# Two weight slabs in turns behind a norm, and where the squares are added: a hybrid encoder on one core

## The chip, the core and the metric

The kernel runs on one core of one Trainium2 chip. The metric is the time of one execution on the device in microseconds (us); the median of several runs is given. The engines are named as the profile names them: PE (TensorE, matrix products; PEld is its loading of weights), DVE (VectorE), ACT (ScalarE), POOL (GpSimd) and SP (SyncE, which issues most transfers).

## The reference

A two-layer encoder over 512 tokens of width 1024, in float32:

```python
def hybrid(x):                                     # [1, 512, 1024]
    x = x + stick_breaking_attention(rms_norm(x, norm_mix[0]), w_qkv, w_o)
    x = x + squared_relu_mlp(rms_norm(x, norm_mlp[0]), mlp_w1[0], mlp_w2[0])
    x = x + rglru_block(rms_norm(x, norm_mix[1]), ...)   # w_in, conv, gates, scan, w_o
    x = x + squared_relu_mlp(rms_norm(x, norm_mlp[1]), mlp_w1[1], mlp_w2[1])
    return rms_norm(x, norm_final)

def rms_norm(x, g):
    return x * rsqrt(mean(x * x, axis=-1) + 1e-6) * g

def squared_relu_mlp(h, w1, w2):                   # w1 1024x4096, w2 4096x1024
    u = relu(h @ w1)
    return (u * u) @ w2
```

## The kernel before, in words

Everything is kept transposed: the stream x is 8 chunks `x[0]` to `x[7]` of 128 channels by 512 tokens. A weight matrix is read in slabs of 1024 inputs by 128 outputs (512 KB). For precision every operand is split into two halves, a rounded one (`wh`, `xgh`, `bh`) and the rest (`wl`, `xgl`, `bl`), and each product is three matmuls (`three`, lines 187 to 191). So one slab (`dense`, line 193) is 8 steps over the chunks k = 0 to 7 with 3 matmuls each, 24 in all, into one PSUM bank.

`slab` (line 168) issues the slab's transfer on SP's queue (line 172), casts `wh` on ACT (line 178) and subtracts `wl` on DVE (line 184). There are four buffers of `wh` and `wl`.

The norm does not stand in front of the next product. `residual` (line 626) finishes the layer: for each chunk c it runs the last slab's product, adds it to `x[c]` (`add_x`, DVE, line 624), writes the halves of x times the norm's gain (`halves`: `xgh` on ACT, line 117; `xgl` on DVE, line 118), and squares the chunk (`Squares.chunk`: Square on ACT, lines 135 and 138, added up into `ssq` on POOL, line 139). Two buffers hold squares. The next layer's first products start from the halves; the factor 1/rms is applied to their results. It comes from `Squares.inv_rms` (line 141): one product of `ssq` with ones on PE (line 143), a square root on ACT and a reciprocal on DVE (lines 123 and 124).

`residual` is called at three seams: attention's end to the first MLP (line 635, gain `mlp0`), the first MLP's end to the recurrent layer (line 824), and the recurrent layer's end to the second MLP (line 1000). At attention's end the products of chunks 0 to 6 are nearly done beforehand (`so`), and only chunk 7 is a whole slab.

The MLP's `squared` (line 675) makes one slab of w1, then scales by `r`, applies the ReLU (DVE, line 684) and squares (ACT, line 685). Its first call also makes `r`, behind its own slab. Two slabs make a pair: four sums on DVE (line 699), a split into halves on ACT (line 715) and DVE (line 716), after which `u`, of one buffer, is free for the next pair. Eight slabs are followed by the first two of the next quarter, and then by `down` (line 736), whose first product reads pairs 0 and 1 (`bh`, `bl`) and then pairs 2 and 3 (`sh`, `sl`). Eight PSUM banks go round in the order `oottaazz`.

The recurrent layer's `dense_in` (line 893) makes one slab of w_in; `conv(0)` calls it first, and that first call makes `r`, behind its own slab.

The order of work: a scheduler orders the instructions of each engine by a priority (program order) and by when its own model takes them to be ready. Inside `manual_schedule(engines={PE})` PE's instructions keep the order in which they are written, but where such a region falls among PE's other instructions stays the scheduler's choice. `high_priority()`, put around each `conv` (line 986), makes instructions come first as soon as they are ready. `issue_after(ins)` queues a block's instructions behind `ins`.

Of the kernel before, what the change touches and what calls it, by code (L numbers as in the profile page):

```python
# [11 lines left out]
F32 = mybir.dt.float32  # L12
F32R = mybir.dt.float32r
AF = mybir.ActivationFunctionType
ALU = mybir.AluOpType
PSUM = bass.MemoryType.PSUM

P = 128
S = 512
D = 1024  # L20
C = D // P
# [26 lines left out]
def hybrid_encoder(  # L48
# [24 lines left out]
    V, A, G, PE = nc.vector, nc.scalar, nc.gpsimd, nc.tensor  # L73
# [3 lines left out]
    work = ctx.enter_context(tc.tile_pool(name="work", bufs=2))  # L77
# [5 lines left out]
    def bank(tag=None):  # L83
        if tag is None:
            tag = TAGS[turn[0] % len(TAGS)]
            turn[0] += 1
        return psum.tile([P, S], F32, tag=tag, name=f"ps_{tag}")

    def f(ap):
        return ap.bitcast(F32)  # L90
# [4 lines left out]
    def col(name):  # L95
        o, n = COLS[name]
        return colt[:, o : o + n]
# [10 lines left out]
    xgh = const.tile([P, C, S], F32R, tag="xgh", name="xgh")  # L108
    xgl = const.tile([P, C, S], F32R, tag="xgl", name="xgl")
# [4 lines left out]
    def halves(gname, c, xc):  # L114

        g = col(gname)[:, c : c + 1]
        A.activation(xgh[:, c, :], xc, AF.Identity, scale=g)  # L117
        V.scalar_tensor_tensor(xgl[:, c, :], xc, g, f(xgh[:, c, :]), ALU.mult, ALU.subtract)  # L118

    def inv_rms(ps):  # L120

# [5 lines left out]
    class Squares:  # L127
# [2 lines left out]
        def __init__(self):  # L130
            self.acc = work.tile([P, S], F32, tag="ssq", name="ssq", bufs=1)

        def chunk(self, c, xc):
            if c == 0:
                A.activation(self.acc, xc, AF.Square)
            else:
                sq = work.tile([P, S], F32, tag="sq", name="sq")
                A.activation(sq, xc, AF.Square)
                G.tensor_tensor(self.acc, self.acc, sq, ALU.add)

        def inv_rms(self):
            ps = bank("z")
# [25 lines left out]
    def slab(src, cut=1, ks=range(C)):  # L168
        raws = rawpools[next(loads) % len(rawpools)]
        raw = raws.tile([P, C, P], F32, tag="raw", name="raw", bufs=3 if raws is wpool else 1)  # L170
        k = slice(ks.start, ks.stop)
        nc.sync.dma_start(out=raw[:, k, :], in_=src[:, k, :])
        pool = wpools[next(slabs) % len(wpools)]
        wh = pool.tile([P, C, P], F32R, tag="wh", name="wh")
        wl = pool.tile([P, C, P], F32R, tag="wl", name="wl")
        for i in range(cut):
            k = slice(ks.start + i * len(ks) // cut, ks.start + (i + 1) * len(ks) // cut)
            A.copy(wh[:, k, :], raw[:, k, :])  # L178
            if adding[0]:

                G.tensor_scalar(wl[:, k, :], f(wh[:, k, :]), -1.0, None, ALU.mult)
                G.dma_start(out=wl[:, k, :], in_=raw[:, k, :], accum_op=ALU.add)
            else:
                V.tensor_tensor(wl[:, k, :], raw[:, k, :], f(wh[:, k, :]), ALU.subtract)  # L184
        return wh, wl

    def three(ps, ah, al, wh, wl, start, stop):

        PE.matmul(ps, wh, ah, start=start, stop=False)  # L189
        PE.matmul(ps, wl, ah, start=False, stop=False)  # L190
        PE.matmul(ps, wh, al, start=False, stop=stop)  # L191

    def dense(src, ah, al, tag=None, halves=None, ks=range(C), ps=None):

        wh, wl = halves or slab(src, ks=ks)
        ps = bank(tag) if ps is None else ps
        for k in ks:
            three(ps, ah[:, k, :], al[:, k, :], wh[:, k, :], wl[:, k, :], k == ks[0], k == ks[-1])
        return ps


    NB = S // P
# [2 lines left out]
    so, early = {}, {}  # L205
# [4 lines left out]
    def home_tile(tag, n, name):  # L210
        return home.tile([P, S], F32, tag=tag, name=name, bufs=n)

    with ExitStack() as actx:
# [19 lines left out]
        for i in range(2):  # L233
            both = []
            for nm in ("h", "l"):
                t = sp.tile([P, 2 * P], F32R, tag=f"last{nm}{i}", name=f"last{nm}{i}")
# [74 lines left out]
        first = [bank("acc") for _ in range(2)]  # L311
# [6 lines left out]
        with tc.manual_schedule(engines=others):  # L318
# [13 lines left out]
            for kind, c in START:  # L332
# [4 lines left out]
                else:  # L337
                    A.activation(sqs[c], xcs[c], AF.Square)
                    if c > 1:
                        e, acc = ((G, sums), (V, odd))[c % 2]  # L340
# [125 lines left out]
        turns = [0]  # L466
# [124 lines left out]
        for i in range(n_fill):  # L591
# [5 lines left out]
            if i == LATE:  # L597
                x = [home_tile(tag, n, "x") for tag, n in HOMES[:7]]
# [16 lines left out]
        for c in range(C - 1):  # L615
            for _ in so_more(c, C - 1):
                pass
            if c == 0:
                so_next = {C - 1: slab(w_so[C - 1], CUT)}
# [3 lines left out]
    def add_x(c, ps):  # L623
        V.tensor_tensor(x[c], x[c], ps, ALU.add)

    def residual(srcs, gname, begun={}, ready={}):

        sq = Squares()
        for c in range(C):
            add_x(c, begun[c][0] if c in begun else dense(srcs[c], bh, bl, halves=ready.get(c)))  # L630
            halves(gname, c, x[c])
            sq.chunk(c, x[c])
        return sq

    sq = residual(w_so, "mlp0", so, so_next)


    NQ = DFF // D
# [3 lines left out]
    class Mlp:  # L642
# [31 lines left out]

        def squared(self, q4, c):

            ps = dense(w_m1[self.layer, q4 * C + c], xgh, xgl, ps=self.bank())
            if self.r is None:
                self.r = self.sq.inv_rms()
            j, a = divmod(c, 2)  # L680
            if a == 0:
                self.u[j] = self.mp.tile([P, PIECES, HS], F32, tag="u", name="u", bufs=1)
            t = self.u[j][:, 2 * a : 2 * a + 2, :].rearrange("p i n -> p (i n)")
            V.scalar_tensor_tensor(t, ps, 0.0, self.r, ALU.max, ALU.mult)  # L684
            A.activation(t, t, AF.Square)  # L685
            return t
# [118 lines left out]
    with ExitStack() as mctx:  # L805
        mctx.enter_context(tc.manual_schedule(engines={mybir.EngineType.PE}))
        mlp = Mlp(mctx, 0, sq)
        back = count()

        def between(q4, c):  # L810

            if q4 < NQ - 1 or c < 4:
                return
            for c in islice(back, 2):
                pt = mlp.bank()
                for t in range(NB):
                    PE.transpose(
                        pt[:, t * P : (t + 1) * P], mlp.y(t, c // 4)[:, c % 4 * P : (c % 4 + 1) * P],
                        ident,
                    )  # L820
                add_x(c, pt)

        mlp.quarters(between)
        sq = residual(w_m2, "mix1")
# [8 lines left out]
    with ExitStack() as rctx:  # L833
# [32 lines left out]
        for i in range(2):  # L866
            t = rp1.tile([P, 2, P], F32, tag=f"graw{i}", name=f"graw{i}")
# [15 lines left out]
        r = None  # L883
# [5 lines left out]

        xc, aa, om, z, hs, gin = {}, {}, {}, {}, {}, {}  # L890
        turns = [0, 0]

        def dense_in(i):

            nonlocal r
            adding[0] = turns[0] >= 6
            ps = dense(w_in[i], xgh, xgl, tag=("acc", "t")[turns[0] % 2])
            turns[0] += 1
            if r is None:
                r = sq.inv_rms()  # L900
            return ps

        def conv(c):

            ps = dense_in(C + c)
            V.tensor_tensor(ps, ps, r, ALU.mult)
            aa[c], xc[c], om[c] = (
                rp1.tile([P, S], F32, tag=t, name=t, bufs=n)
                for t, n in (("aa", 5), ("bt", 6), ("om", C))
            )  # L910
            x0 = xc[c]
            nonlocal begin, tap, high, low
            taps = [cw[:, i * C + c : i * C + c + 1] for i in range(4)]
            begin = A.activation(x0, ps, AF.Identity, bias=col("conv_b")[:, c : c + 1], scale=taps[3])
            for d in range(1, 4):
                tap = V.scalar_tensor_tensor(
                    x0[:, d:], ps[:, : S - d], taps[3 - d], x0[:, d:], ALU.mult, ALU.add
                )

            i = C - 3 + c % 3  # L920
            xch, xcl = bh[:, i, :], bl[:, i, :]
            high = A.copy(xch, x0)
            low = V.tensor_tensor(xcl, x0, f(xch), ALU.subtract)
            gin[c] = (xch, xcl, *gate_weights(c))
# [39 lines left out]
        def gate(c):  # L964
            ps = dense_in(c)
            z[c] = rp1.tile([P, S], F32, tag="z", name="z", bufs=6)
            V.tensor_tensor(z[c], ps, r, ALU.mult)
# [23 lines left out]
        begun = {}  # L991
        for c in range(4):
            wh, wl = slab(w_ro[c])
            begun[c] = bank("oozz"[c]), wh, wl
        for k in range(C):
            for c in range(4):
                ps, wh, wl = begun[c]
                three(ps, bh[:, k, :], bl[:, k, :], wh[:, k, :], wl[:, k, :], k == 0, k == C - 1)

    sq = residual(w_ro, "mlp1", begun)  # L1000
    wctx.close()
    wpools[:], rawpools[:] = [wpool], [wpool]


    with ExitStack() as mctx:
# [24 lines left out]
        for h in range(2):  # L1030
            ws = []
            for k in range(C // 2):
                raw = wpool.tile([P, C, P], F32, tag="raw", name="raw", bufs=3)
                nc.sync.dma_start(out=raw, in_=w_last[h, k])
                wh = lw.tile([P, C, P], F32R, tag="wh", name="wh")
                A.copy(wh, raw)
                wl = lw.tile([P, C, P], F32R, tag="wl", name="wl")
                V.tensor_tensor(wl, raw, f(wh), ALU.subtract)
                ws.append([t.rearrange("p (k f) e -> p k (f e)", k=2) for t in (wh, wl)])
            for t in range(NB):  # L1040
# [3 lines left out]
                for i, (e0, e1) in enumerate(units):  # L1044
                    ps = bank()[:, : e1 - e0]
                    for k in range(C):
                        wh, wl = (w[:, k % 2, e0:e1] for w in ws[k // 2])
# [4 lines left out]
                    g = gb[:, h * S + e0 : h * S + e1]  # L1052
# [11 lines left out]
                last = len(units)  # L1064
# [83 lines left out]
```

## Time and profile before

| what | value |
|---|---|
| runs, us | 1099.35, 1099.39, 1102.22 |
| median, us | 1099.39 |
| profiled execution, us | 1099.0 |
| its span, us | 1097.3 |
| mean granted clock of PE | 0.996 |
| PE / DVE / ACT / POOL busy, us | 1075.0 / 772.1 / 563.4 / 216.7 |

The span runs from the first to the last instruction of the profiled execution. A timeline row gives the start, the duration, the engine, the line of the kernel, the operation and what it writes and reads, and in brackets the idle time before it and what ended that. Matmuls are pipelined: a row's duration is from issue to end, so the distance of two starts is what one costs. A row of the list of waits gives who waited for whom: us in total, times, the longest. A row of busy time by stretch gives the stretch, its length, and each engine's busy time with the number of instructions, then PE's granted clock, the share of the DMA engines and GB/s.

### The profile page before, as it was taken

To read this page: it belongs to the slowest core of one execution; us is meant where nothing else is said; L and a number is where in the kernel's file an instruction comes from. 1 tells how busy PE (TensorE), PEld (TensorE's weight loads), DVE (VectorE), ACT (ScalarE), POOL (GpSimd) and SP (SyncE) were. 2 spreads that over 40 slices of the span, in tenths; PEclk is the share of its full clock that TensorE was granted. 3 is DMA by queue.
4 is the path that set the end of the run, shared out by engine and by line. 5 is a ranking of instruction groups with operands and counts; after the bars stand their busy time and mean duration, and the time that the engine had idled before them with its cause. 6 is when DMAs were issued, how large, how long until landed. Compare 5 with 4: busy or idle time off the path is not lost.

```text
span 1097.3 us, 13621 instructions
## 1 busy us (share of the span) xinstructions
PE 1075.0 (98%) x5052; PEld 890.0 (81%) x5052; DVE 772.1 (70%) x986; ACT 563.4 (51%) x831; POOL 216.7 (20%) x228
## 2 busy tenths in 40 slices
PE   9999999998999999999999999999999999999997
PEld 7888888886888888888888788888888888888886
DVE  7777787838784597699565648975684697699522
ACT  6766776726445444344344467854455444443422
POOL 2344344533000000000222555122000000002220
PEclk9999999999999999999999999999999999999999
DMA  7744354436205305301334476242205205303402
GB/s 236 196 108 136 103 147 107 137 100 216 94 20 173 116 20 171 116 20 56 118 108 135 103 183 144 96 168 90 88 31 183 95 22 186 99 1 103 165 1 77
DMA packets 43170, 122.57 MB, mean 112 GB/s; under 512 B 7648, under 2 KB 8416, under 8 KB 43104
## 3 DMA queue, kind: packets, MB, share of 16 engines
q1 hardware_dynamic: 41088, 115.94, 33.9%
q0 software_dynamic: 1440, 5.24, 2.6%
q8 instruction: 40, 0.66, 0.2%
q10 hardware_dynamic: 576, 0.52, 0.2%
q14 instruction: 26, 0.21, 0.1%
HBM read 101.76 MB, written 2.10 MB: 95 GB/s over the span
## 4 chain that ended last, share of the span: by engine, by line
PE 91%; DVE 4%; DMA 2%; ACT 1%; issue 1%; SPq 1%; POOL 0%; DVEq 0%; ACTq 0%; POOLq 0%
PE ps_acc L189 7%; PE ps_acc L190 7%; PE ps_acc L191 7%; PE ps_o L191 4%; PE ps_t L190 4%; PE ps_t L189 4%; PE ps_t L191 4%; PE ps_o L189 4%; PE ps_o L190 4%; PE ps_z L190 3%; PE ps_z L189 3%; PE ps_z L191 3%; PE ps_t L758 2%; PE ps_t L757 2%; PE ps_t L759 2%; PE ps_acc L758 2%
## 5 line engine op out<-in xcount | busy, mean ns | idle before, releaser
L178 ACT CAST wh<-raw 128x1024 fp32r<-128x1024 f32 (+2 forms) x144 | 128.4, 910 | 156.0 <-PE ps_acc L191 51.3
L184 DVE TENSOR_TENSOR wl<-raw,wh 128x1024 fp32r<-128x1024 f32 (+2 forms) x134 | 146.0, 1103 | 30.9 <-ACT wh L178 30.8
L690 POOL TENSOR_TENSOR bl<-u,bh 128x512 fp32r<-128x512 f32 x16 | 28.2, 1761 | 559.4 <-ACT bh L689 541.5
L189 PE MATMUL ps_acc<-xgh,wh 128*128 128x512 f32 x320 | 128.3, 401 | 1.3 <-ACT xgh L117 1.1
L732 ACT CAST wh<-b 128x1024 fp32r<-128x1024 f32 x72 | 75.5, 1049 | 102.4 <-PE ps_acc L759 16.2
L191 PE MATMUL ps_acc<-xgl,wh 128*128 128x512 f32 x320 | 125.8, 393 | 0.6 <-DVE xgl L118 0.6
L190 PE MATMUL ps_acc<-xgh,wl 128*128 128x512 f32 x320 | 126.0, 394 | 0.2 <-DVE wl L160 0.2
L733 DVE TENSOR_TENSOR wl<-b,wh 128x1024 fp32r<-128x1024 f32 x72 | 87.9, 1221 | 27.1 <-ACT wh L732 27.1
L493 DVE TENSOR_TENSOR_SCAN scan<-keep,later 128x128 f32<-128x128 f32 (+1 forms) x64 | 56.9, 890 | 22.9 <-ACT keep L485 14.4
L191 PEld LDWEIGHTS ps_acc<-xgl,wh 128*128 128x128 f32 x320 | 60.4, 189 | 14.6 <-DVE xgl L118 1.5
L189 PEld LDWEIGHTS ps_acc<-xgh,wh 128*128 128x128 f32 x320 | 60.5, 189 | 12.8 <-ACT xgh L117 1.8
L190 PEld LDWEIGHTS ps_acc<-xgh,wl 128*128 128x128 f32 x320 | 60.5, 189 | 10.8 <-DVE wl L160 0.8
L685 ACT ACTIVATE u<-u 128x512 f32<-128x512 f32 x64 | 39.6, 630 | 54.4 <-DVE u L684 54.2
L189 PE MATMUL ps_t<-xgh,wh 128*128 128x512 f32 x168 | 66.1, 394 | 0.0
L497 POOL TENSOR_TENSOR w<-w,scan 128x128 f32<-128x128 f32 (+1 forms) x64 | 54.9, 858 | 56.4 <-DVE scan L493 55.0
L190 PE MATMUL ps_t<-xgh,wl 128*128 128x512 f32 x168 | 65.7, 391 | 0.0
L191 PE MATMUL ps_t<-xgl,wh 128*128 128x512 f32 x168 | 65.5, 390 | 0.0
L191 PE MATMUL ps_o<-xgl,wh 128*128 128x512 f32 x152 | 60.3, 397 | 3.9 <-DVE xgl L118 3.9
L189 PE MATMUL ps_o<-xgh,wh 128*128 128x512 f32 x152 | 61.1, 402 | 0.0
L190 PE MATMUL ps_o<-xgh,wl 128*128 128x512 f32 x152 | 59.7, 393 | 0.0
L189 PE MATMUL ps_z<-xgh,wh 128*128 128x512 f32 x128 | 50.0, 391 | 0.0
L190 PE MATMUL ps_z<-xgh,wl 128*128 128x512 f32 x128 | 49.9, 390 | 0.0
(339 smaller groups left out, 2783.4 us busy)
## 6 DMA issues: line engine op xcount, KB each, us to landing
raw<-in_w_m SPq DMA_DIRECT2D x72, 512.0 KB, 3.5
b<-in_w_dn SPq DMA_DIRECT2D x36, 512.0 KB, 4.3
raw<-in_w_in SPq DMA_DIRECT2D x16, 512.0 KB, 3.5
raw<-in_w_qk SPq DMA_DIRECT2D x12, 512.0 KB, 3.8
raw<-in_w_dn SPq DMA_DIRECT2D x12, 512.0 KB, 3.5
wl<-raw POOLq DMA_DIRECT2D x10, 512.0 KB, 5.3
x<-in_xT SPq DMA_DIRECT2D x16, 256.0 KB, 4.1
raw<-in_w_ro SPq DMA_DIRECT2D x8, 512.0 KB, 3.5
```

Source lines behind the costliest of these rows:

```text
L178: A.copy(wh[:, k, :], raw[:, k, :])
L184: V.tensor_tensor(wl[:, k, :], raw[:, k, :], f(wh[:, k, :]), ALU.subtract)
L189: PE.matmul(ps, wh, ah, start=start, stop=False)
L190: PE.matmul(ps, wl, ah, start=False, stop=False)
L191: PE.matmul(ps, wh, al, start=False, stop=stop)
L493: V.tensor_tensor_scan(sc[:, S - n : S][:, ::-1], keep[:, :n][:, ::-1], later[:, S - n :][:, ::-1], 1.0, ALU.mult, ALU.max,)
L497: G.tensor_tensor(wt, wt, sc[:, S - n + 1 : S + 1], ALU.mult)
L685: A.activation(t, t, AF.Square)
L690: G.tensor_tensor(bl[:, c, :], t, f(bh[:, c, :]), ALU.subtract)
L732: A.copy(wh, raw)
L733: V.tensor_tensor(wl, raw, f(wh), ALU.subtract)
L758: PE.matmul(ps[i], h[:, piece, ts], wl[:, jj, :], start=False, stop=False)
```

## The change

A new helper, `beside`, loads several slabs and runs their products step by step in turns: step k of the first, step k of the second, then step k + 1. If it is given the sum of squares, it makes `r` just before step 4, which is after 24 matmuls of two slabs.

In the first MLP, the first two slabs of w1 go through `beside`, the third through `dense`, and `r` is made behind the third. In the second MLP and in the recurrent layer (the slabs of `conv(0)` and `conv(1)`), the first two slabs go through `beside` with the sum, so `r` is made between steps 3 and 4.

At attention's end (`burst=True`) the squares are no longer taken chunk by chunk. All chunks' halves are written first; then the eight chunks are squared and added, with seven buffers for squares in place of two, and with POOL's additions inside `issue_after` of the last chunk's `xgl`. The diff, cut to its core:

```diff
         A.activation(xgh[:, c, :], xc, AF.Identity, scale=g)
-        V.scalar_tensor_tensor(xgl[:, c, :], xc, g, f(xgh[:, c, :]), ALU.mult, ALU.subtract)
+        return V.scalar_tensor_tensor(
+            xgl[:, c, :], xc, g, f(xgh[:, c, :]), ALU.mult, ALU.subtract
+        )
...
-        def chunk(self, c, xc):
+        def chunk(self, c, xc, last=None, pool=None):
             if c == 0:
                 A.activation(self.acc, xc, AF.Square)
             else:
-                sq = work.tile([P, S], F32, tag="sq", name="sq")
+                sq = (pool or work).tile([P, S], F32, tag="sq", name="sq")
                 A.activation(sq, xc, AF.Square)
-                G.tensor_tensor(self.acc, self.acc, sq, ALU.add)
+                with tc.issue_after(last.ins) if last is not None else nullcontext():
+                    G.tensor_tensor(self.acc, self.acc, sq, ALU.add)
...
+    def beside(srcs, ah, al, pss, sq=None):
+
+        ws = [slab(src) for src in srcs]
+        for k in range(C):
+            if k == 4 and sq is not None:
+                r = sq.inv_rms()
+            for ps, (wh, wl) in zip(pss, ws):
+                three(ps, ah[:, k, :], al[:, k, :], wh[:, k, :], wl[:, k, :], k == 0, k == C - 1)
+        return r if sq is not None else None
...
-    def residual(srcs, gname, begun={}, ready={}):
+    def residual(srcs, gname, begun={}, ready={}, burst=False):
...
-            halves(gname, c, x[c])
-            sq.chunk(c, x[c])
+            last = halves(gname, c, x[c])
+            if not burst:
+                sq.chunk(c, x[c])
+        if burst:
+
+            with tc.tile_pool(name="squares", bufs=C - 1) as pool:
+                for c in range(C):
+                    sq.chunk(c, x[c], last, pool)
         return sq
 
-    sq = residual(w_so, "mlp0", so, so_next)
+    sq = residual(w_so, "mlp0", so, so_next, burst=True)
...
         def squared(self, q4, c):
 
-            ps = dense(w_m1[self.layer, q4 * C + c], xgh, xgl, ps=self.bank())
             if self.r is None:
-                self.r = self.sq.inv_rms()
+                self.first = [self.bank() for _ in range(2)]
+                srcs = [w_m1[self.layer, i] for i in range(3)]
+                if self.layer == 0:
+
+                    beside(srcs[:2], xgh, xgl, self.first)
+                    self.first.append(dense(srcs[2], xgh, xgl, ps=self.bank()))
+                    self.r = self.sq.inv_rms()
+                else:
+                    self.r = beside(srcs[:2], xgh, xgl, self.first, self.sq)
+            if self.first:
+                ps = self.first.pop(0)
+            else:
+                ps = dense(w_m1[self.layer, q4 * C + c], xgh, xgl, ps=self.bank())
...
         def dense_in(i):
 
             nonlocal r
             adding[0] = turns[0] >= 6
-            ps = dense(w_in[i], xgh, xgl, tag=("acc", "t")[turns[0] % 2])
+            if r is None:
+                first.extend(bank(t) for t in ("acc", "t"))
+                r = beside([w_in[C], w_in[C + 1]], xgh, xgl, first, sq)
             turns[0] += 1
-            if r is None:
-                r = sq.inv_rms()
-            return ps
+            if first:
+                return first.pop(0)
+            return dense(w_in[i], xgh, xgl, tag=("t", "acc")[turns[0] % 2])
```

More of the change, by code (lines that the diff above doesn't have):

```diff
@@ L891, in hybrid_encoder @@
         turns = [0, 0]
+        first = []
         def dense_in(i):
```

## The prediction

> **What bounds the kernel now.** I read the page first, then the list of waits of the tensor engine (PE), then the timeline of every engine around the three seams where a layer's last residual slab meets the next layer's first slab, and last a table of busy time by stretch.
>
> ```profile
> span 1097.3 us, 13621 instructions
> PE 1075.0 (98%) x5052; PEld 890.0 (81%) x5052; DVE 772.1 (70%) x986; ACT 563.4 (51%) x831; POOL 216.7 (20%) x228
> ...
> PE ps_t L509 <- DVE tl L523: 5.6, 4, 2.1
> PE ps_o L191 <- DVE xgl L118: 3.9, 4, 1.9
> ...
> PE ps_acc L189 <- ACT xgh L117: 1.1, 1, 1.1
> ...
> PE ps_z L143 <- POOL ssq L139: 0.6, 1, 0.6
> PE ps_acc L191 <- DVE xgl L118: 0.6, 1, 0.6
> ```
>
> PE is busy for 98% of the span, so nothing but PE's own gaps can be won. The list names few: 5.6 us lie in attention (L509), which the change leaves alone; those on `xgl`, `xgh` and the sum of squares (L143) lie at the seams that the change edits. What an unbroken slab costs shows at the last seam, from the first matmul of a slab of 24 to the sum behind it (0.227 us for one matmul):
>
> ```profile
> 751.57 0.39 PE L189 MATMUL ps_o<-xgh,wh 128*128 128x512 f32 x1
> ...
> 757.01 1.02 PE L143 MATMUL ps_z<-ssq,ones 128*128 128x512 f32 x2
> ```
>
> So 5.44 us per slab. Against that stands the seam behind attention (PE, then DVE and POOL, then the table by stretch: length, busy us of PE, PEld, DVE, ACT, POOL, clock):
>
> ```profile
> 258.20 0.39 PE L189 MATMUL ps_o<-xgh,wh 128*128 128x512 f32 x1
> ...
> 266.36 0.80 PE L191 MATMUL ps_o<-xgl,wh 128*128 128x512 f32 x1 [1.91 <-DVE xgl L118]
> ...
> 270.09 1.12 PE L143 MATMUL ps_z<-ssq,ones 128*128 128x512 f32 x2
> ...
> 276.54 0.39 PE L189 MATMUL ps_t<-xgh,wh 128*128 128x512 f32 x1
> ...
> 257.11 1.21 DVE L184 TENSOR_TENSOR wl<-raw,wh 128x1024 fp32r<-128x1024 f32 x1
> 258.25 5.17 DVE L118 SCALAR_TENSOR_TENSOR xgl<-x,colt,xgh 128x512 fp32r<-128x512 f32 x3
> 263.34 2.30 DVE L184 TENSOR_TENSOR wl<-raw,wh 128x1024 fp32r<-128x1024 f32 x1
> 265.56 0.74 DVE L118 SCALAR_TENSOR_TENSOR xgl<-x,colt,xgh 128x512 fp32r<-128x512 f32 x1
> ...
> 266.82 2.06 DVE L118 SCALAR_TENSOR_TENSOR xgl<-x,colt,xgh 128x512 fp32r<-128x512 f32 x3
> ...
> 259.80 4.75 POOL L139 TENSOR_TENSOR ssq<-ssq,sq 128x512 f32<-128x512 f32 x3 [0.32 <-ACT sq L138]
> ...
> 258.20:270.09 11.89, 7.95 (x26) 4.86 (x24) 11.63 (x11) 4.79 (x8) 7.59 (x5) 0.86 0.76 294
> 266.00:269.40 3.40, 3.04 (x8) 2.29 (x9) 3.14 (x6) 2.18 (x3) 1.08 (x1) 0.53 0.50 157
> ```
>
> The slab takes 11.89 us instead of 5.44: 6.45 us lost. DVE makes three `xgl` in 5.17 us while POOL adds squares, and three in 2.06 us once POOL is quiet. PE waits on each, and its clock falls to 0.53 behind the longest gap.
>
> **The seam behind attention.** The change makes the first two slabs share the chunks: step k now feeds six matmuls (1.36 us) instead of three. The 48 matmuls need 10.88 us; done in that time, the pair would save all 6.45 us. The bounds come from when `xgl` lands. Chunk 4's `xgl` let PE go on at 266.36; in the pair it is due at 258.20 + 4 x 1.36 + 2 x 0.227 = 264.09. If DVE's times stay, PE is 2.27 late and the gain is 4.2. If only the weight half at 263.34 (the third slab's, not needed before 269) falls behind the `xgl`, chunk 3 decides: it ends at 258.25 + 5.17 = 263.42, due at 262.73, 0.7 late, gain 5.75. The new cost is that the second slab's `wl` is due early, at 259.1; here it ended at 257.11 + 1.21 = 258.32, but with POOL running beside it (2.30 instead of 1.21) or with squares ahead of its cast on ACT it comes up to 3 us late, gain 3.4. I take 4.8, between the first two, as the sum matmul also moves behind a third slab and the squares no longer wait for a buffer that POOL must free.
>
> The wording "added up behind the halves" I do not count on. The helper `issue_after` draws order edges only to instructions of the engine of the instruction it is given; that one is DVE's `xgl`, the adds are POOL's, so it should draw none. What is left is ACT's order: squares come behind the `xgh` when both are ready, and seven buffers let them run on. POOL keeps adding beside DVE. ACT's and POOL's totals do not change (row: 21 adds, median 1612 ns, as low as 1282).
>
> ```profile
> L139 POOL TENSOR_TENSOR ssq<-ssq,sq x21: 1282/1612/1782, 254.2 to 754.1; 128x512 f32<-128x512 f32 x21
> L118 DVE SCALAR_TENSOR_TENSOR xgl<-x,colt,xgh x32: 737/746/1876, 5.7 to 754.0; 128x512 fp32r<-128x512 f32 x32
> ```
>
> The second row says the same of DVE: 746 ns at the median, 1876 at worst.
>
> **What comes late then: 1/rms.** In layer 0 the sum matmul stands behind the third slab, so `r` comes later against PE's progress.
>
> ```profile
> 273.35 3.35 DVE L124 RECIPROCAL r<-r 128x512 f32<-128x512 f32 x1 [0.78 <-ACT r L123]
> 276.81 1.29 DVE L684 SCALAR_TENSOR_TENSOR u<-ps_o,r 128x512 f32<-128x512 f32 x2
> ...
> 282.51 2.02 DVE L716 TENSOR_TENSOR bl<-u,bh 128x1792 fp32r<-128x1792 f32 x1 [1.81 <-ACT bh L715]
> ...
> 309.37 0.69 DVE L684 SCALAR_TENSOR_TENSOR u<-ps_z,r 128x512 f32<-128x512 f32 x1 [0.40 <-PE ps_z L191]
> ...
> 318.30 2.02 DVE L716 TENSOR_TENSOR sl<-u,sh 128x1792 fp32r<-128x1792 f32 x1
> ...
> 320.06 0.39 PE L757 MATMUL ps_t<-wh,bh 128*128 128x512 f32 x1
> ...
> 322.79 0.39 PE L757 MATMUL ps_t<-wh,sh 128*128 128x512 f32 x1
> ```
>
> The sum starts at 258.20 + 72 x 0.227 + 1.65 (what of the 6.45 is not won) = 276.2; `r` follows 6.6 later, as from 270.09 to 276.70, so at 282.8. All eight banks are there for the slabs, so PE runs on. But `u` has one buffer, so four pairs of slabs pass one by one through DVE and ACT: 276.81 to 284.53 is 7.7 for the first, 309.37 to 320.32 is 10.95 for the last, which shares DVE with the next stage's weights. The first down matmul would stand at 276.2 + 1.0 (the sum: 6.45 from 270.09 to 276.54, less a slab) + 7 x 5.44 = 315.3, and the last pair's halves are due 3.4 later (2.73 to the first `sh`, three matmuls more), at 318.7. Two pairs at 7.7 and two at 10.95 end at 320.1, 1.4 late; four at 7.7 end at 313.7, no wait. I take -0.5.
>
> **The seam into the recurrent layer.** This seam is not like the first:
>
> ```profile
> 598.14 0.39 PE L189 MATMUL ps_acc<-xgh,wh 128*128 128x512 f32 x1
> ...
> 602.34 0.40 PE L191 MATMUL ps_acc<-bl,wh 128*128 128x512 f32 x1
> ...
> 608.05 0.39 PE L189 MATMUL ps_acc<-xgh,wh 128*128 128x512 f32 x1
> ...
> 612.41 1.12 PE L143 MATMUL ps_z<-ssq,ones 128*128 128x512 f32 x2 [0.63 <-POOL ssq L139]
> ...
> 610.58 1.77 POOL L139 TENSOR_TENSOR ssq<-ssq,sq 128x512 f32<-128x512 f32 x1 [3.69 <-DVE wl L184]
> ...
> 608.05:612.41 4.36, 2.10 (x8) 0.86 (x6) 2.58 (x3) 2.79 (x4) 1.77 (x1) 1.00 0.17 65
> ```
>
> `conv` has top priority, so the scheduler already put 18 of the first slab's matmuls (k = 0 to 5) ahead of the end of the residual; six were left to fill the 4.36 us in which the last chunk is squared and added (to 610.58 + 1.77 = 612.35). In the change the sum stands ahead of step 4 in PE's fixed order. So 24 matmuls (four steps of two slabs) can go ahead and none is left: PE must stand still until the sum. The last residual slab ends 6 x 0.227 = 1.36 later, the sum comes 4.36 after it as before, and 24 matmuls follow it in both kernels. That is -1.36, with no part given back. A gap of 4.36 without a matmul may also lower the clock: the 3.40 us at 0.53 above lost 1.6, while this stretch with its six matmuls kept 1.00. Between 0 and 1.6 I take 1.0, as the gap is longer and emptier than the 1.91 that came before the 0.53. Together -2.4.
>
> **The seam into the second MLP.**
>
> ```profile
> 754.11 1.78 POOL L139 TENSOR_TENSOR ssq<-ssq,sq 128x512 f32<-128x512 f32 x1 [3.66 <-ACT sq L138]
> 752.86 1.22 DVE L184 TENSOR_TENSOR wl<-raw,wh 128x1024 fp32r<-128x1024 f32 x1 [0.40 <-ACT wh L178]
> ```
>
> PE has no gap here. The sum keeps its place behind 24 matmuls, at 757.01, and the squares are done at 755.89. The second slab's weights were cast two slabs earlier by the order of their four buffers. Cost 0; if the half at 752.86 were that slab's, PE would wait from 752.25 to 754.08, 1.8.
>
> **Sum.** +4.8 - 0.5 - 2.4 + 0 = 1.9 us saved. The profiled execution took 1099.0 (span 1097.3 and 1.7 around it), so 1097.1; it lies 0.4 below the median of 1099.39, so the median becomes 1097.5. With the ends (3.4 - 1.4 - 3.0 and 6.45 - 0 - 1.36) the likeliest case spans -1.0 to +5.1: 1100.4 to 1094.3.
>
> **Rivals.** (1) The pair is not pulled ahead at the recurrent seam. Then the last residual slab ends 18 x 0.227 = 4.08 earlier, at 603.97, its sum is ready 4.36 later, at 608.3, and 24 matmuls cover that: the sum starts at 609.4, 3.0 earlier than 612.41. Net +4.8 - 0.5 + 3.0 = 7.3, 1092.1. For it: step 0 needs two slabs' weights now, and I know only the order of one. Against it: 18 went ahead in a row, which is what chunks 0 to 5 allow. Chance 0.17.
>
> (2) Slower: the four pairs of `u` decide. If each takes 10.95 (DVE is 70% busy and the next stage's additions fill its gaps), the last ends at 282.8 + 43.8 = 326.6, 7.9 behind 318.7. Net 4.8 - 7.9 - 2.4 = -5.5, 1104.9. It decides from 9.0 us per pair (35.9 / 4). Against it: before the down stage's weights come up, a pair took 7.7. Chance 0.10.
>
> (3) The adds do wait for the last `xgl`. Then DVE is free of POOL and the seam gives 6.45, less up to 0.8 if seven adds of 1.28 to 1.61 from about 264 reach past the sum at 274.5: 6.0 - 0.5 - 2.4 = 3.1, 1096.3. Chance 0.08.
>
> (4) The clock stays at half for the whole of a 3.40 stretch behind the gap at the recurrent seam: 1.36 + 1.6, net 4.8 - 0.5 - 3.0 = 1.3, 1098.1. The row with 0.53 speaks for it, the row with 1.00 for the main case. The Trainium skill ("TensorE: Matmul & The Clock Gate", Part 1) halves the clock after an idle window of about 3.4 us until a window is busy; by it an estimate is 1.7 lost. The trace agrees only in part: its dip came after gaps of at most 1.91. Chance 0.15.
>
> **How the numbers follow.** The forecast keeps 0.50, at 1097.5. What a measurement can tell from no change I put at 0.3%, 3.3 us (the three runs lie within 2.9). Faster by more: rival 1 (0.17), a fifth of the main case (0.11), half of rival 3 (0.05): 0.33. Slower by more: rival 2, and 0.03 of the main case for a late second slab at the last seam: 0.13. Within: 0.54. The range goes from rival 1's time to the slow end of the main case, 1092.0 to 1100.4; rival 2 and the better half of rival 1 are left out.
>
> **What would show it.** Right: from PE's first `xgh` matmul behind attention, 48 matmuls in 11 to 13 us with no clock near 0.5; `xgl` still above 1.5 us beside POOL; 24 `xgh` matmuls ahead of the last residual slab before the recurrent layer, then a PE gap of about 4 us on `ssq`; a sum in layer 0 near 276. Wrong: a PE wait on `sl` or `u` at the first down stage over 2 us (rival 2), or no gap on `ssq` at the recurrent seam (rival 1).

## The result, and the profile after

The changed kernel takes 1107.49 us (median of 5, 1106.35 to 1110.23); the kernel before, on the same chip, 1099.35 (1098.47 to 1102.22). The ratio is 1.0075 with a 95% interval of 1.0055 to 1.0095: slower, by about 0.75%. The forecast of 1097.5 was wrong, and so was its range. The profiled execution took 1106.35, with a span 7.3 longer than before.

From the page and the list of PE's waits of the changed kernel (line 194 is line 191 of before, 146 is 143; 787 and 789 are two of the three matmuls of `down`):

```profile
span 1104.6 us, 13619 instructions
PE 1076.9 (97%) x5052; PEld 891.5 (81%) x5052; DVE 771.5 (70%) x986; ACT 563.3 (51%) x831; POOL 219.7 (20%) x228
...
PE ps_t L787 <- ACT sh L745: 4.4, 1, 4.4
PE ps_z L146 <- POOL ssq L142: 4.2, 1, 4.2
PE ps_o L194 <- DVE xgl L118: 2.2, 1, 2.2
...
PE ps_t L789 <- DVE sl L746: 1.0, 1, 1.0
```

The busy times hardly moved. The waits did: of `xgl` behind attention one is left of four, and two new ones have come, 4.4 + 1.0 on the halves of the last pair of `u` (`sh`, `sl`) and 4.2 on the sum of squares. The timeline shows each in its place. First the seam behind attention, PE, then DVE, POOL and the busy time by stretch:

```profile
257.88 0.39 PE L192 MATMUL ps_o<-xgh,wh 128*128 128x512 f32 x1
...
266.50 0.51 PE L194 MATMUL ps_o<-xgl,wh 128*128 128x512 f32 x1 [2.24 <-DVE xgl L118]
...
271.62 0.39 PE L192 MATMUL ps_t<-xgh,wh 128*128 128x512 f32 x1
...
277.07 1.02 PE L146 MATMUL ps_z<-ssq,ones 128*128 128x512 f32 x2
...
257.35 5.19 DVE L118 SCALAR_TENSOR_TENSOR xgl<-x,colt,xgh 128x512 fp32r<-128x512 f32 x3
262.47 2.30 DVE L187 TENSOR_TENSOR wl<-raw,wh 128x1024 fp32r<-128x1024 f32 x1
...
265.29 4.19 DVE L118 SCALAR_TENSOR_TENSOR xgl<-x,colt,xgh 128x512 fp32r<-128x512 f32 x4
...
255.05 10.85 POOL L142 TENSOR_TENSOR ssq<-ssq,sq 128x512 f32<-128x512 f32 x6 [10.30 <-ACT sq L140]
...
258.00:272.00 14.00, 11.76 (x51) 9.04 (x50) 12.61 (x10) 5.37 (x9) 9.06 (x6) 1.00 0.68 258
```

The pair takes 271.62 - 257.88 = 13.74 us for 48 matmuls, with one wait and the clock at 1.00. POOL's additions run from 255.05, beside the `xgl`; they are not held until the last one. So far the seam did what was said. Then the first down stage: DVE's `r`, then three steps of the chain through `u` (its first, the start of the third pair at 302.20, its last), with the first work for the down weights (lines 763 and 780) among them; then PE, and the clock (columns as in the front part):

```profile
280.39 3.35 DVE L126 RECIPROCAL r<-r 128x512 f32<-128x512 f32 x1 [0.78 <-ACT r L125]
283.86 1.29 DVE L714 SCALAR_TENSOR_TENSOR u<-ps_o,r 128x512 f32<-128x512 f32 x2
...
301.06 1.22 DVE L763 TENSOR_TENSOR wl<-b,wh 128x1024 fp32r<-128x1024 f32 x1
302.20 1.28 DVE L714 SCALAR_TENSOR_TENSOR u<-ps_acc,r 128x512 f32<-128x512 f32 x2
303.40 1.21 DVE L780 TENSOR_TENSOR b<-b,b 128x1024 f32<-128x1024 f32 x1
...
323.98 2.03 DVE L746 TENSOR_TENSOR sl<-u,sh 128x1792 fp32r<-128x1792 f32 x1 [0.67 <-ACT sh L745]
...
316.05 0.39 PE L787 MATMUL ps_t<-wh,bh 128*128 128x512 f32 x1
...
324.00 0.65 PE L787 MATMUL ps_t<-wh,sh 128*128 128x512 f32 x1 [4.36 <-ACT sh L745]
...
326.06 0.79 PE L789 MATMUL ps_t<-wh,sl 128*128 128x512 f32 x1 [0.98 <-DVE sl L746]
326.65 0.63 PE L787 MATMUL ps_t<-wh,sh 128*128 128x512 f32 x1
327.08 0.63 PE L788 MATMUL ps_t<-wl,sh 128*128 128x512 f32 x1
...
363.46 0.40 PE L192 MATMUL ps_o<-xgh,wh 128*128 128x512 f32 x1
...
324.19:331.01 6.82, 5.84 (x14) 4.05 (x14) 4.63 (x7) 3.16 (x5) 0.00 (x0) 0.50 0.00 0
```

The last pair's split ends at 326.01, and PE, at the down stage since 316.05, stands still for it. Behind the gap the clock is 0.50 for 6.82 us, and matmuls come every 0.43 us until 330.9. The row at 363.46 is the next w1 slab behind this stage; before it stood here:

```profile
358.98 0.40 PE L189 MATMUL ps_o<-xgh,wh 128*128 128x512 f32 x1
```

Three starts in PE's timeline now measure layer 0 in every kernel, free of what lies ahead of it: the first `xgh` matmul behind attention, the first down matmul, and that slab.

| kernel | three starts | seam to down | down stage |
|---|---|---|---|
| before | 258.20, 320.06, 358.98 | 61.86 | 38.92 |
| after | 257.88, 316.05, 363.46 | 58.17 | 47.41 |

The seam gains 3.69 and the down stage loses 8.49. These lengths repeat well: in the seven profiled kernels that have this pair with the squares and additions as here, the first one is 58.17 to 58.25, and where nothing waits the down stage takes 38.92 or 38.93. Third, the seam into the recurrent layer:

```profile
602.62 0.39 PE L192 MATMUL ps_acc<-xgh,wh 128*128 128x512 f32 x1
...
618.24 2.08 PE L146 MATMUL ps_z<-ssq,ones 128*128 128x512 f32 x2 [4.17 <-POOL ssq L142]
...
626.17 0.39 PE L192 MATMUL ps_acc<-xgh,wh 128*128 128x512 f32 x1
...
618.00:622.00 4.00, 3.76 (x9) 2.37 (x10) 0.93 (x1) 0.69 (x1) 0.18 (x1) 0.61 0.23 84
```

From the first `xgh` matmul that was pulled ahead to the end of the two slabs it takes 626.17 - 602.62 = 23.55. Before, the same work took 618.85 - 598.14 = 20.71 to this row:

```profile
618.85 0.39 PE L189 MATMUL ps_acc<-xgh,wh 128*128 128x512 f32 x1
```

Lost: 2.84. The seam into the second MLP has no wait. 3.69 - 8.49 - 2.84 = -7.64; with the 0.32 by which the first start lies earlier (257.88, 258.20) this is the span's -7.3.

### The profile page after: what moved, and what is told of

It reads as the page before. It is cut to its first block, busy times and chain, and to the rows that moved or that the text cites. A ratio compares the mean times of both kernels' runs of the same rounds, so it can differ in the third digit from the quotient of the medians.

```text
span 1104.6 us, 13619 instructions
## 1 busy us (share of the span) xinstructions
PE 1076.9 (97%) x5052; PEld 891.5 (81%) x5052; DVE 771.5 (70%) x986; ACT 563.3 (51%) x831; POOL 219.7 (20%) x228
## 4 chain that ended last, share of the span: by engine, by line
PE 90%; DVE 4%; DMA 2%; ACT 2%; issue 1%; POOL 0%; SPq 0%; DVEq 0%; ACTq 0%; POOLq 0%
PE ps_acc L192 7%; PE ps_acc L193 7%; PE ps_acc L194 7%; PE ps_t L193 4%; PE ps_t L192 4%; PE ps_t L194 4%; PE ps_o L194 4%; PE ps_o L192 4%; PE ps_o L193 4%; PE ps_z L193 3%; PE ps_z L192 3%; PE ps_z L194 3%; PE ps_t L789 2%; PE ps_t L788 2%; PE ps_t L787 2%; PE ps_acc L787 2%
## 5 line engine op out<-in xcount | busy, mean ns | idle before, releaser
L720 POOL TENSOR_TENSOR bl<-u,bh 128x512 fp32r<-128x512 f32 x16 | 31.5, 1968 | 562.3 <-ACT bh L719 546.4
L510 POOL TENSOR_TENSOR w<-w,scan 128x128 f32<-128x128 f32 (+1 forms) x64 | 51.7, 809 | 56.8 <-DVE scan L506 55.4
```

Source lines behind the costliest of these rows:

```text
L510: G.tensor_tensor(wt, wt, sc[:, S - n + 1 : S + 1], ALU.mult)
L720: G.tensor_tensor(bl[:, c, :], t, f(bh[:, c, :]), ALU.subtract)
```

## The experiments

Two theories. **A:** the three places are independent, and layer 0 loses because the late `r` starts the chain of four pairs through `u` too late for the first down stage. **Rival:** the places hang together, or something else in the change (the squares' order, the seam, DVE's load as such) makes the loss. Times are medians; each ratio is to the kernel before on the same chip.

**1. Layer 0's part alone.** The recurrent layer's and the second MLP's edits are taken back.

> Only the first MLP's part of the change is kept (pair, sum behind the third slab, squares in a burst); the recurrent layer and the second MLP are as before. Theory A (two separate losses: the pairs of u decide the first down stage, 8.4 us of wait and slow clock, against 3.6 us won at the seam; and 2.8 us at the recurrent seam): 4.8 us above the kernel before, so about 1104.2, the wait on sh and sl at the first down matmuls stays at 5.4 us, the wait for the sum at the recurrent seam falls from 4.2 to about 0.6 us. Theory B (taking slabs in turns costs in each layer that has it, because two slabs hold their weight buffers at once): about a third of the loss stays, 1101.5 to 1102.5.

1104.99 us, ratio 1.0044 (1.0029 to 1.0059); the same 4.4 us on `sh`, and 0.6 on `ssq`, as expected. Layer 0 is slower by itself.

**2. The recurrent part alone.** `burst=True` and both MLPs' edits are taken back.

> The kernel before with the recurrent layer's part of the change alone. Theory A (the parts add up; the recurrent seam loses what the change's own trace shows, 23.55 us instead of 20.71): 1100.1 + 2.8 = 1102.9 us, a wait of about 4.2 us on ssq at the seam, none at the first down stage. Rival (the wait is an effect of the later time at which the residual stage comes in the changed kernel): within 1 us of the kernel before.

1102.8, ratio 1.0035 (1.0022 to 1.0048), with 4.2 on `ssq` and none at the down stage. The two parts add up (0.0044 + 0.0035 = 0.0079, against 0.0075 for the whole change), so the loss has two separate places, and nothing is left over for the second MLP.

**3. The late sum alone.** No pairs anywhere; only the place of layer 0's sum is changed, from behind the first slab to behind the third. Cut to its core, against the kernel of experiment 2, whose first MLP works as before:

```diff
-                    self.first = [dense(srcs[0], xgh, xgl, ps=self.bank())]
+                    self.first = [dense(s, xgh, xgl, ps=self.bank()) for s in srcs]
                     self.r = self.sq.inv_rms()
```

> The kernel before, with no pairs at all: only layer 0's sum of squares is moved from behind the first slab to behind the third. Theory A (the place of the sum by itself costs what the first down stage lost): r comes two slabs, 10.9 us, later, at about 287.6; the four pairs of u at 10.5 each end at 329.7, and the first down stage, which starts at 320 as before, waits for the halves of the last pair, 5 to 9 us with the slow matmuls behind the gap: about 7 us slower than before, 1104 to 1108. Rival (the late sum hurts only because the pair of slabs brings PE to the down stage 3.7 us sooner, and with the chain at 38 us the lateness is 2 us): 1 to 4 us slower, 1100 to 1103.

1108.13, ratio 1.0073 (1.0051 to 1.0094). DVE's `r` and last split, and PE's waits:

```profile
286.18 3.35 DVE L126 RECIPROCAL r<-r 128x512 f32<-128x512 f32 x1 [0.78 <-ACT r L125]
...
329.81 2.03 DVE L744 TENSOR_TENSOR sl<-u,sh 128x1792 fp32r<-128x1792 f32 x1 [0.67 <-ACT sh L743]
...
PE ps_t L785 <- ACT sh L743: 4.4, 1, 4.4
```

Starts 259.77, 321.88, 369.05: the seam takes 62.11, as before, and the down stage 47.17, 8.25 more than before. The whole loss is there with no pair and no burst; the time lies 0.1 above the expected end. What the two kernels share is how far `r` lies ahead of the first down matmul: 32.35 here (289.53, 321.88), 32.31 in the changed kernel (283.74, 316.05), but 43.36 before (276.70, 320.06). The rival (1 to 4 us) falls.

**4. The sum early.** The change, with layer 0's sum straight behind the pair and the third slab, made as all later ones, after it:

```diff
                     beside(srcs[:2], xgh, xgl, self.first)
-                    self.first.append(dense(srcs[2], xgh, xgl, ps=self.bank()))
                     self.r = self.sq.inv_rms()
```

> The change, but in the first MLP the sum of squares stands straight behind the pair, ahead of the third slab. Theory A: r comes 5.4 us earlier (about 278.3 instead of 283.7), the last pair's halves with it (about 320.6 instead of 326.0, due at 319.5): the wait at the first down matmuls falls from 5.4 to at most 1.5 us and the clock stays up, so the time falls by 6.5 to 8.4 us, to 1099 to 1101. The squares' sum was complete at 268.3 in the change, before the pair ended at 271.6, so the sum itself waits for nothing. Theory C (DVE fills whatever room there is with the next stage's additions, so that the pairs end late whenever r comes): the wait stays over 3 us and the time above 1104.

1098.2, ratio 0.9986 (0.9975 to 0.9997), better than expected. DVE's `r`, the chain's first and last step, and PE's first matmul on `sh`:

```profile
275.11 3.35 DVE L126 RECIPROCAL r<-r 128x512 f32<-128x512 f32 x1 [0.59 <-ACT r L125]
278.57 1.29 DVE L713 SCALAR_TENSOR_TENSOR u<-ps_o,r 128x512 f32<-128x512 f32 x2
...
314.72 2.02 DVE L745 TENSOR_TENSOR sl<-u,sh 128x1792 fp32r<-128x1792 f32 x1
...
318.68 0.39 PE L786 MATMUL ps_t<-wh,sh 128*128 128x512 f32 x1
```

`sh` and `sl` are ready 1.9 us ahead of PE (316.74 against 318.68), and the down stage takes 38.93 (starts 257.73, 315.95, 354.88), as before. `r` came 5.28 sooner than in the changed kernel, but the chain's end 9.27 sooner: the chain takes 38.2 us instead of 42.1. The additions for the down weights (line 780 above, 779 here), which DVE puts between the chain's steps, come up at about the same time in both (the first at 303.40 there, 302.17 here), and the later `r` is, the more of them the chain meets: seven there, five here, and five subtractions for these weights against three.

**5. The additions held.** The change, with the down weights' additions of the first quarter queued on DVE behind the last split, which `self.low` names:

```diff
-            V.tensor_tensor(l, u, f(h), ALU.subtract)
+            self.low = V.tensor_tensor(l, u, f(h), ALU.subtract)
...
-                        V.tensor_tensor(raw, raw, self.raws[to, g], ALU.add)
+                        held = self.layer == 0 and q4 == 0
+                        with tc.issue_after(self.low.ins) if held else nullcontext():
+                            V.tensor_tensor(raw, raw, self.raws[to, g], ALU.add)
```

> The change, but in the first MLP's first quarter the additions that make the down stage's combined weights are queued on DVE behind the last pair's split. Theory A with its cause in DVE's order: the four pairs took 42.1 us, of which 10 were additions and casts between their steps; with these held they take about 33 (two at 7.7, two at 8.5 to 9), so that the last ends near 317.5 and the first down matmuls wait at most 0.5 us; the additions come later and may cost 0 to 2 us at the second product. Time 1099 to 1101.5. If it is only the late start that decides and not the order: the last split still ends after 323, the wait stays over 3 us, time above 1104.

1102.04, ratio 1.0016 (1.0002 to 1.003), 0.5 above the expected end. The chain takes 33.6 us (284.66 to 318.28), the waits on `sh` and `sl` are gone, and in their place the weights are late (1.3 and 0.9 on `wl`, line 790). So with `r` just as late (284.54, 32.31 ahead of the first down matmul) the stage loses only 41.62 - 38.92 = 2.7 (starts 258.61, 316.85, 358.47). It is the late `r` together with DVE's order that makes the 8.5.

**6. The additions truly behind the halves.** A one-column read of the last `xgl` is put on POOL, ahead of its additions:

```diff
+                mark = pool.tile([P, 1], F32, tag="mark", name="mark", bufs=1)
+                last = G.tensor_scalar(mark, f(xgl[:, C - 1, :1]), 1.0, None, ALU.mult)
                 for c in range(C):
```

> The change, with a one-column read of the last xgl put on POOL ahead of the additions, so that these do wait for it. Theory A (DVE is slowed by POOL's additions beside it; 1/rms then sets when the first down stage may begin): the eight xgl take 0.7 us each instead of 1.4 to 1.8, the pair of slabs has no wait and ends about 2.3 us sooner, r comes at 281 to 283 as seven additions now follow the last xgl; so the first down stage still waits 4 to 7 us, and the time is 1105 to 1107.5. Rival (the seam behind attention, not r, is what the end hangs on): 2.3 to 2.6 us gained whole, 1104 or less, with no longer wait at the down stage.

1105.34, ratio 1.0055 (1.0042 to 1.0068). DVE, POOL, then PE's first matmul of the pair and of the third slab:

```profile
256.07 2.07 DVE L118 SCALAR_TENSOR_TENSOR xgl<-x,colt,xgh 128x512 fp32r<-128x512 f32 x3
...
259.79 2.74 DVE L118 SCALAR_TENSOR_TENSOR xgl<-x,colt,xgh 128x512 fp32r<-128x512 f32 x4
...
262.97 12.09 POOL L142 TENSOR_TENSOR ssq<-ssq,sq 128x512 f32<-128x512 f32 x7
...
257.10 0.39 PE L192 MATMUL ps_o<-xgh,wh 128*128 128x512 f32 x1
...
267.98 0.39 PE L192 MATMUL ps_t<-xgh,wh 128*128 128x512 f32 x1
```

Three `xgl` take 2.07 us instead of 5.19, and the pair runs in 267.98 - 257.10 = 10.88, without a gap. But the sum now waits 1.5 for the additions, the seam gains only 1.09 more (57.08; starts 257.10, 314.18, 361.92), and the down stage still waits (4.4 and 1.3): 47.74. `r` was done at 280.35, a little ahead of the 281 to 283 expected.

**7. No burst.** `burst=True` is dropped, the squares stand behind each chunk's halves.

> The change without its last part: each chunk's squares and addition stand behind that chunk's halves, as before. Theory A (the additions were never held, so the part moves ACT's order alone): within 1.5 us of the changed kernel, 1106 to 1109; wait on the halves of the last pair at the down stage 3 to 6 us. Rival (the seven buffers and the order of the squares are what makes 1/rms late): the wait at the down stage goes and the time is 1101 or less.

1106.57, ratio 1.0065 (1.0053 to 1.0077). Seam 57.72, down stage 47.52 (258.40, 316.12, 363.64). The burst does nothing good here: the seam is 0.45 better without it, and the two times cannot be told apart (1.0055 to 1.0095 with it).

**8. The recurrent layer's sum behind step 7.** `r` is made after the loop of `beside` instead of ahead of step 4.

> The change, but in the recurrent layer the sum stands behind step 7 of the pair instead of before step 4. Theory A (what counts at this seam is how many matmuls are left to lie in the 4.4 us while the last chunk is squared and added): 42 matmuls go ahead of the residual's end and six are left, as many as in the kernel before, so the seam costs what it cost there: 2.8 us less than the change, about 1104.7, with a wait for the sum of 2 to 3 us and no clock near 0.5. Theory B (the pair itself costs at this seam): no change, 1107.5.

1109.17, ratio 1.008 (1.0061 to 1.0098): a miss, 4.5 above the expected time. The wait on `ssq` is gone, but two slabs later the gates wait instead (PE, line 968 and 970 are the gates' matmuls):

```profile
635.82 0.50 PE L968 MATMUL ps_o<-bh,gh 128*128 128x512 f32 x1 [1.66 <-ACT bh L957]
...
638.23 0.80 PE L970 MATMUL ps_o<-bl,gh 128*128 128x512 f32 x1 [1.68 <-DVE bl L958]
```

Here `r` is done at 628.7, 7 us ahead of the first gate's start; before it was 11.7 ahead (618.2 and 629.9). Behind the first of them the clock is 0.51, from 637 to 644. It looks like layer 0 again: PE does not need `r` at once, but a chain on DVE and ACT hangs on it. This is read from the trace; no run isolated it.

**9. Layer 0 as in 4, the rest as before.**

> Layer 0's two slabs take turns, its sum stands straight behind the pair, and the recurrent layer and the second MLP are as before. Theory A (the gain of the seam behind attention stays, no wait at the down stage, no gap at the recurrent seam): the 1098.2 measured with the recurrent part, less its 2.8, so 1095.4 us. Rival (the recurrent part costs nothing by itself): 1098.

1095.85, ratio 0.9967 (0.9954 to 0.9979): faster than the kernel before. Starts 258.73, 316.94, 355.87: 58.21 and 38.93.

**10. The recurrent pair behind the residual.** As 4, but `beside` is called ahead of the list of chunks, outside `conv`'s high priority, and no longer in `dense_in`:

```diff
+        first.extend(bank(t) for t in ("acc", "t"))
+        r = beside([w_in[C], w_in[C + 1]], xgh, xgl, first, sq)
         for what, c in (
```

> As the kernel with layer 0's sum straight behind the pair (measured 1098.2 us), but the pair of the recurrent layer is formed ahead of the list of its chunks, without their high priority, so that PE's fixed order has all 48 matmuls behind the last residual slab. Theory A (the 4.2 us on ssq come from matmuls that were pulled ahead and so are missing behind the last chunk; this is the prediction's first rival, 3.0 gained against the kernel before): no wait on ssq at that seam, 1098.2 - 2.8 - 3.0 = 1092.4 us. Rival (a late r, not the missing matmuls, decides, as where the sum stood behind step 7): gates wait again, 1095 or more.

1092.21, ratio 0.9923 (0.9905 to 0.994): as expected, and the fastest version. PE at the seam, and busy time by stretch:

```profile
601.02 0.39 PE L192 MATMUL ps_acc<-xgh,wh 128*128 128x512 f32 x1
...
606.62 1.02 PE L146 MATMUL ps_z<-ssq,ones 128*128 128x512 f32 x2
...
590.00:625.00 35.00, 35.00 (x152) 28.22 (x151) 21.72 (x25) 15.35 (x20) 15.56 (x8) 1.00 0.25 67
```

All 48 matmuls stand behind the last residual slab, 24 of them cover the squares of the last chunk, and PE has no gap in 35 us. So the wait came from the matmuls that had been pulled ahead and were missing behind the last chunk.

**11 and 12. Both holds.** The edits of 5 and 6 in layer 0, with the recurrent layer as before (11) and as in 10 (12).

> The change with POOL's additions held behind the last xgl (measured 1105.34 us by itself), the down stage's additions of the first quarter held behind the last split (worth 6.5 by itself), and the recurrent layer and the second MLP as before (worth 3.05). Theory A (each loss has its own place and they add up): 1105.3 - 6.5 - 3.0 = 1095.8 us, no wait on the halves at the first down stage. Rival (with r earlier against PE by only 0.7 the held additions come late and PE waits on wl instead): 2 us or more in waits on wl, 1098 or more.

> Both holds in layer 0, and the recurrent layer's pair behind the last residual slab. Theory A: the sum of the two, 1095.8 - 3.0 = 1092.8 us. Rival as in those: 1096 or more.

1098.59, ratio 0.9991 (0.9979 to 1.0002), and 1094.92, ratio 0.9953 (0.9939 to 0.9967): 2.8 and 2.1 above theory A. In 11 both signs of the rival came, 1.3 and 0.9 on `wl` and a time above 1098; but experiment 5 had the same two waits, so they are already in the hold's price. Layer 0 shows 57.08 and 41.61 (258.90, 315.98, 357.59), 2.09 better than before. So I had set the hold 0.4 too high (47.74 - 41.61 = 6.1, not 6.5). In the profiled execution another 1.6 goes at the recurrent seam, which has the same matmuls in the same order as before, and the same waits on `xgh`, `xgl` and `ssq` (1.1, 0.6, 0.6):

```profile
596.75 0.39 PE L192 MATMUL ps_acc<-xgh,wh 128*128 128x512 f32 x1
...
619.07 0.39 PE L192 MATMUL ps_acc<-xgh,wh 128*128 128x512 f32 x1
...
611.41:614.82 3.41, 3.41 (x8) 2.13 (x7) 1.32 (x1) 2.02 (x3) 2.94 (x2) 0.50 0.08 30
```

From the first `xgh` matmul to the end of the two slabs it takes 619.07 - 596.75 = 22.32 where the kernel before took 20.71, because the clock is at half for 3.41 us. What makes up 12's 2.1 is open. Making `r` early (10) beats holding what stands in its way (12) by 2.7.

## Why the prediction was wrong, step by step

**The seam behind attention, +4.8: it gave 3.69.** The mechanism was right. "If DVE's times stay, PE is 2.27 late": the one wait was 2.24. They stayed, and the value for that case, 4.2, should have been the forecast; 4.8 leaned on a weight half that did not move (262.47, between the `xgl`, as before). The pair took 13.74, 0.6 more than 10.88 + 2.27, so even 4.2 was a little high, and "48 matmuls in 11 to 13 us" was missed by that much. The new cost, a late `wl` of the second slab, did not come. That the additions are not held was right, too. Experiment 6 shows what holding them gives: 4.78.

**"I take -0.5" for the late `r`: it cost 8.49.** This is the step that failed, and with it the sign. The rest of its arithmetic held: `r` at 283.74 (said 282.8), the first down matmul at 316.05 (said 315.3). What failed is the length of the chain through `u`. The middle case added two pairs at 7.7 and two at 10.95, 37.3 in all, with the end at 320.1. In the changed kernel the pairs took 7.7, 8.5, 10.4 and 12.4, with 1.05 between one and the next, 42.1 in all, and the end came at 326.01. Of these 5.91 us, 1.06 are the chain's later start, 3.16 the three gaps, which the sum left out (in each DVE does one `wl` subtraction of 1.22), and 1.69 longer pairs.

That two pairs would be slow was right. Before, the work for the down weights began behind the third pair:

```profile
306.03 1.22 DVE L733 TENSOR_TENSOR wl<-b,wh 128x1024 fp32r<-128x1024 f32 x1
307.17 0.68 DVE L684 SCALAR_TENSOR_TENSOR u<-ps_z,r 128x512 f32<-128x512 f32 x1
```

In the changed kernel it begins at 301.06, ahead of the third (302.20), so the third and the fourth meet it. But 10.95 was not a whole pair: it was counted from 309.37, the second of two scalings by `r`, the first of which, at 307.17, was done while PE still made the second slab. The last pair took 12.4; and the second took 8.5, with a `wl` subtraction of w1 among its sums.

The prediction also put no clock on this gap. Of the 8.49, 5.34 are the two waits; the 6.82 us at half clock, less the 0.98 of waiting in them, lose half of 5.84, which is 2.9, and so nearly all the rest. The Trainium skill ("TensorE: Matmul & The Clock Gate", Part 1) gives 426.7 ns from start to start for N = 512 at half clock; the trace agrees (326.65 to 327.08, 0.43).

Rival (2) is what happened: it named the chain and the wait on `sl`. Its numbers, 43.8 for the chain and 7.9 for the loss, came near 42.1 and 8.49 partly by luck: it had four slow pairs without gaps, and a loss that was all waiting. It stood at 0.10 because a pair that meets no down weights took 7.7. The quoted rows had a warning: from 276.81 to 320.32 the whole chain of before took 43.5 us. Part of that was waiting for PE's slabs, but nothing in the profile showed that it could be done in 31; with the additions held (experiment 5) it still took 33.6.

**The recurrent seam, -2.4: it cost 2.84.** Right: 24 `xgh` matmuls ahead of the last residual slab's end, then 4.17 on `ssq`. Of the 2.84, 1.36 is the missing cover, and 1.48 is left for the slow clock, between the 1.0 I took and rival (4)'s 1.6; the stretch shows 0.61, and from the sum to the end of the two slabs it is 7.93 (618.24 to 626.17) where before it was 6.44. But "this stretch with its six matmuls kept 1.00" rested on one execution. Four other profiled kernels have the same matmuls in the same order at this seam (experiments 1, 3, 9 and 11), and in all four the clock fell to half there: they took 22.34, 22.31, 23.42 and 22.32 where the kernel before took 20.71. Against these the change's 23.55 is only 0.1 to 1.2 more. So how much of the 1.48 belongs to the change stays open; the times of experiment 2 (3.05 more than before) speak for all of it.

Rival (1), the pair not pulled ahead, did not occur, but experiment 10 built it. It saves 6.65 (1098.86 to 1092.21) where the rival had 7.3. Of that, 3.6 come from layer 0 (starts 259.02, 317.27, 356.20, so 58.25 and 38.93), where the rival had 4.3, and 3.05 are left for the recurrent seam, where it had 3.0. That the time itself, 1092.21, lies so near the rival's 1092.1 is partly luck.

**The second MLP, 0:** right, no wait in the list.

**What would show it wrong:** "a PE wait on `sl` or `u` at the first down stage over 2 us" came, as 4.4 on `sh`, `sl`'s twin.

## What to carry to other kernels

A factor that PE does not need for its next products can still be the head of a chain that PE needs later: when its place moves, follow the chain to the first product that reads its end, and take its length whole, from the first step to the last, with the gaps, not as a number of its best steps. A chain that shares its engine with work that comes at a time of its own can get longer the later it starts: here 5.3 us sooner at the head were 9.3 at the end. And taking two slabs in turns uses up matmuls that cover the last chunk: count what is left to do when the sum is due, and keep the scheduler from pulling it ahead. Last, read the clock behind a gap from more than one execution: the one profile that the prediction had showed 1.00 where four others showed half.

## What the runs showed of the hardware

POOL's additions and DVE's operations with two operands in SBUF slow each other. Three `xgl` took 5.19 us beside additions and 2.07 without (experiment 6), 1.73 against 0.69 each. The additions lengthen as well. Two of the seven in experiment 6, with the `wl` subtraction that DVE began while the first of them ran, and one addition of the changed kernel beside its `xgl`:

```profile
264.34 1.29 POOL L142 TENSOR_TENSOR ssq<-ssq,sq 128x512 f32<-128x512 f32 x1
265.42 1.29 DVE L187 TENSOR_TENSOR wl<-raw,wh 128x1024 fp32r<-128x1024 f32 x1 [2.89 <-ACT wh L181]
265.71 2.16 POOL L142 TENSOR_TENSOR ssq<-ssq,sq 128x512 f32<-128x512 f32 x1
...
260.38 1.62 POOL L142 TENSOR_TENSOR ssq<-ssq,sq 128x512 f32<-128x512 f32 x1
```

In experiment 6 the three additions that began while a `wl` subtraction ran took 2.15 to 2.16 us, the other four 1.27 to 1.30. The Trainium skill ("SBUF — State Buffer", section "SBUF: two separate sides") says that of a DVE operation with two SBUF inputs and a POOL operation the later one is blocked until the other ends. The trace agrees in both directions: what began second is what took longer, and beside a run of additions DVE gets about one `xgl` through per addition.

The granted clock fell for stretches of about 3.4 or 6.8 us, and it did not follow the longest gap alone. Four waits of 0.6 to 1.9 us behind attention brought half clock for 3.41 us in all three profiled kernels that have them (before, experiments 2 and 3), and one wait of 2.24 left 1.00 in the changed kernel. The gap of 4.36 at the down stage brought 6.82 us at half clock, the one of 4.17 at the recurrent seam 3.42. The same gaps need not give the same clock, as the recurrent seam of the kernel before shows: its waits of 1.1, 0.6 and 0.6 us left 1.00 in its own profile and brought half clock for 3.41 us in experiment 11; in experiment 9, with 1.1, 0.6 and 0.3, it was 6.83.
